# A hybrid decoder block with a planned instruction order: other durations in the planner, and late operands on TensorE

## Chip, cores and metric

One Trainium2 chip, one core. The metric is the time of one execution on the device in microseconds (us); less is better. Engines are called as the profile calls them: PE is TensorE, DVE is VectorE, ACT is ScalarE, POOL is GpSimd, SP is SyncE (it only issues DMAs here).

## What is computed

One layer over 1024 tokens of width 1024, in float32, cut to its steps:

```python
xn = rms_norm(x, norm1_g)
q, k, v, p_rw = split(xn @ w_in)                # one input projection, 3328 columns
attn = dilated_attention(q, k, v, ...)          # 8 heads of 64: three dilations, softmax merged
attn = rms_norm(attn, attn_out_g)
rwkv = rwkv7_time_mix(p_rw, ...)                # 8 heads of 64: a state of 64x64 per head, by token
x = x + concatenate([attn, rwkv]) @ w_out
xn2 = rms_norm(x, norm2_g)
return x + (silu(xn2 @ w_gate) * (xn2 @ w_up)) @ w_down     # hidden width 2816
```

## The kernel before

Matmuls with large operands are made from three products of halves: each operand is split into a high part and the rest (ACT writes `inhi`, `oph`, `woh`, ..., DVE or POOL `inlo`, `opl`, `wol`), and PE sums high x high, high x low, low x high.

The work has four stages that overlap. (1) x is loaded, normed and transposed (`xn0h`, `xn0l`, ...). (2) The input projection, `inproj`, goes through 26 column blocks for two halves of the tokens; `feed` takes each result out of PSUM. For q and k it squares (`sqf`) and scales (`qs`) with ACT, transposes the squares on PE to sum them, spreads the factors back (`exf`) and stores to DRAM (`qh_d`, `kh_d`, ...); v goes by `vf`. Beside it runs the RWKV part for eight units n (a pair of heads, half of the tokens), as streams: `decays`, `keys`, `scoring`, `sides`, `turn`, `invert`, `merge`, `chain` and `post`. `chain` is serial: for each of 8 chunks of 64 tokens in each unit (64 steps in all) PE multiplies by the state (S,ra), DVE copies the result to `Rb` (two copies), PE multiplies (Rb,M), DVE copies to `VS` and ACT to `Ub` (two copies), PE multiplies (VS,kbT and Ub,M), DVE makes the new state S (two operations), ACT reads Y out. `post` norms a unit's Y and stores it to `mix_d`; for the last unit it does so in two halves and mostly on DVE. (3) Attention: `attn_load` fetches `qv`, `kk` and `bias` for one of 16 visits to a head (two buffers), workers `attend` make scores (kk,qv), softmax (`sb`), transposes (cs,sb) and values (pt,vv). The output projection has two rounds: the first takes the RWKV results (`mixr` from `mix_d`, four of the eight row blocks of w_out, loaded by `fetch_wo` as `woraw`), the second the attention results. (4) The feed-forward part: gate and up projections and a down projection, 2928 matmuls.

No engine's order is written by hand. Each stream is a generator that yields its operations with a rank; `Flow` is a list scheduler that runs while the program is built and keeps a clock per engine (`self.clk`), and for each tile buffer when each engine will have written or read it. `ready` says when a stream's next operation could start: the engine's clock, or the end of the operations that it depends on plus a lag for the engine that they ran on (`LAG`; 60 ns more if it is to run on PE). `run` takes the operation that is ready first; among those ready by now, the one of lowest rank. `scan` estimates an operation's duration (`op.cost`) from its engine and size. `chain` has rank 3, the other RWKV streams 3.1 to 3.6, `inproj` 9: input projection matmuls are what PE does when nothing else is ready. What is planned is recorded at once in each engine's program, and on the chip each engine takes its own in that order, waiting for its operands.

What the planner may choose from also depends on where the program stands. The streams of `attn_load` are there from the start, but `fetch_wo`, `mix_load`, `mix_T` and `outproj` are added after `flow.run(rwkv)`, when every RWKV stream including `post` has been planned to its end, and the attention workers after `flow.run(dense)`, when the input projection has too:

```python
flow.run(rwkv)
...
ph3 = [flow.add(3.8, fetch_wo()), flow.add(7.4, load_wo()), flow.add(7.5, mix_load()), ...]
flow.run(dense)
...
attn += [flow.add(8.2 + 0.01 * w, attend(w)) for w in range(NW)]
```

All instructions are issued through `emit`, so every row of the profile shows that one line, and the tiles tell them apart.

Of the kernel before, what the change touches and what calls it, by code (L numbers as in the profile page):

```python
# [44 lines left out]
NFIX = C_MASK  # L45


LAG = {"PE": 200, "ACT": 145, "DVE": 140, "POOL": 65, "SP": 900}

OWN = {"PE": 0, "ACT": 100, "DVE": 130, "POOL": 95, "SP": 900}  # L50


# [4 lines left out]
class Op:  # L57


    def __init__(self, eng, name, fn, a, k):  # L60
        self.eng, self.name, self.fn, self.a, self.k = eng, name, fn, a, k
# [40 lines left out]
class Flow:  # L102
# [4 lines left out]
    def __init__(self):  # L107
        self.now, self.clk, self.marks, self.streams = 0.0, {}, {}, []
        self.slots, self.keys, self.count, self.shared = {}, {}, {}, set()
        self.free, self.weights = {}, 0.0  # L110

    def tile(self, pool, shape, dtype, name, tag=None, bufs=1):
        tag = tag or name
# [13 lines left out]
    def scan(self, op):  # L127

        def size(ap):
            n = 1  # L130
            for d in ap.shape[1:]:
                n *= d
            return n

        args = [("out" if i == 0 else "in", v) for i, v in enumerate(op.a)] + list(op.k.items())
        aps = [(k, v) for k, v in args if hasattr(v, "tensor")]
        op.wr = [self.keys[v.tensor.name] for k, v in aps if k in ("out", "accum_out") and v.tensor.name in self.keys]
        op.rd = [self.keys[v.tensor.name] for k, v in aps if k not in ("out", "accum_out") and v.tensor.name in self.keys]
        op.wr += [k for k in op.rd if k[0] in self.shared]
        n = max(size(v) for k, v in aps)  # L140
        ptr = sum(hasattr(op.k.get(k), "tensor") for k in ("scale", "bias", "scalar", "scalar1"))
        if op.eng == "PE":
            if op.name == "transpose":
                op.cost, op.m = 110, 128
            else:
                n, m, k = size(op.k["out"]), size(op.k["lhsT"]), op.k["lhsT"].shape[0]
                passes = 1 if op.k["lhsT"].dtype != F32 else PASSES if max(m, k) <= 64 else 4
                op.cost, op.m = 0.4167 * n * passes + 3, m
        elif op.eng == "SP":
            op.cost = 0  # L150
            op.bytes = 4 * max(size(v) * v.shape[0] for k, v in aps)
        elif op.eng == "POOL":
            op.cost = (280 if op.k.get("op") == ALU.pow else 100) + 93 * ptr + n * (168 if op.k.get("op") == ALU.pow else
                                            {"tensor_tensor": 2.15, "tensor_copy": 3.4}.get(op.name, 1.1))
        elif op.eng == "ACT":
            op.cost = 95 + 0.83 * n + 93 * ptr + 91 * ("accum_out" in op.k)
        else:
            op.cost = 65 + 1.04 * n + 64 * ptr

    def advance(self, s):  # L160
        while s.head is None and not s.done:
# [14 lines left out]
    def ready(self, s):  # L176
        op = s.head
        if isinstance(op, Wait):
            if any(m not in self.marks for m in op.marks):
                return None  # L180
            return max((self.marks[m] for m in op.marks), default=0.0)
        if isinstance(op, Get):
            t, n = sorted(self.free[op.kind].values()), op.n or 1
            return t[n - 1] if len(t) >= n else None
        r = self.clk.get(op.eng, 0.0)
        if op.eng == "SP":
            r = max(r, self.clk.get("queues", 0.0) - 3000)
        for keys, which in ((op.rd, 0), (op.wr, 0), (op.wr, 1)):
            for k in keys:
                if k in self.slots:  # L190
                    for e, t in self.slots[k][which].items():
                        if e != op.eng or (e == "SP" and (keys is op.rd or which)):
                            r = max(r, t + LAG[e] + (60 if op.eng == "PE" else 0))
                        elif keys is op.rd and which == 0:
                            r = max(r, t + OWN[e])
        return r

    def issue(self, s, r):
        op = s.head
        s.head = None  # L200
        if isinstance(op, Wait):
            return
        if isinstance(op, Get):
            free = self.free[op.kind]
            s.gift = sorted(free, key=free.get)[:op.n or 1]
            for tag in s.gift:
                del free[tag]
            if op.n is None:
                s.gift = s.gift[0]
            return  # L210
        start = max(r, self.now)
        if op.eng == "SP":
            self.clk["SP"] = start + 475
            end = max(start + 1125, self.clk.get("queues", 0.0)) + op.bytes / 360
            self.clk["queues"] = end
        else:
            if op.eng == "PE":

                start = max(start, self.weights + 0.833 * op.m)
                self.weights = start  # L220
            self.clk[op.eng] = end = start + op.cost
        for keys, which in ((op.rd, 1), (op.wr, 0)):
            for k in keys:
                self.slots.setdefault(k, ({}, {}))[which][op.eng] = end
        s.t = end + (LAG["SP"] if op.eng == "SP" else 0)
        self.emit(op)
# [1611 lines left out]
```

## Time and profile before

| | |
|---|---|
| median of 3 runs | 1495.26 us (1494.31 to 1502.86) |
| the profiled execution, own time | 1502.63 us |
| its span, first to last instruction | 1500.8 us |
| PE busy | 1420.0 us (95%) |
| DVE, ACT, POOL busy | 803.8, 712.8, 541.8 us |
| DMA queue q1 | 172.26 MB, 38.7% of 16 engines |
| granted PE clock, mean | 0.986 |

Busy time is summed by engine; a matmul's record overlaps the next one's, so a row's mean duration is longer than the step from one matmul to the next. A wait is idle time of an engine before an instruction, put down to what came last.

### The profile page before, as it was taken

What the parts mean: (1) busy time and instruction counts of PE and PEld (TensorE: products, weight loads), DVE (VectorE), ACT (ScalarE), POOL (GpSimd) and SP (SyncE); (2) the same over time, 40 slices, a digit from 0 to 9 for tenths busy, and PEclk for the clock granted to TensorE, in tenths of its full rate; (3) what the DMA queues carried; (4) which work ended last, traced back from release to release, by engine and by line L of the source; (5) the groups of instructions that cost most, each with busy time, mean ns of one, the idle gap of its engine ahead of it and who ended that gap; (6) DMA issues with size and microseconds to landing.
All of it is one profiled execution on the core that took longest, in us unless ns stands there. A gap on an engine that the chain in (4) does not pass through costs nothing.

```text
span 1500.8 us, 24737 instructions
## 1 busy us (share of the span) xinstructions
PE 1420.0 (95%) x8710; PEld 1142.2 (76%) x8710; DVE 803.8 (54%) x1795; ACT 712.8 (47%) x1764; POOL 541.8 (36%) x564
## 2 busy tenths in 40 slices
PE   8899999999898998899899799999999999999999
PEld 6666766677676776788777688888888888888887
DVE  4456577765655345667687744344443444334334
ACT  6434646556667766557666533333333333333332
POOL 5432344345454455133436734444444440000000
PEclk9899999999999999999999899999999999999999
DMA  6242232331422338996813222222222223445443
GB/s 201 85 128 65 67 82 78 79 96 54 126 82 89 104 116 255 249 243 159 197 37 106 73 90 83 79 78 79 79 82 85 78 85 134 147 146 198 148 147 127
DMA packets 199789, 173.83 MB, mean 116 GB/s; under 512 B 39025, under 2 KB 150897, under 8 KB 199666
## 3 DMA queue, kind: packets, MB, share of 16 engines
q1 hardware_dynamic: 199666, 172.26, 38.7%
q8 instruction: 69, 1.13, 0.3%
q14 instruction: 54, 0.44, 0.1%
HBM read 130.26 MB, written 37.75 MB: 112 GB/s over the span
## 4 chain that ended last, share of the span: by engine, by line
PE 54%; DMA 4%; DVE 3%; SPq 1%; ACT 1%; issue 1%; POOL 0%; ACTq 0%; POOLq 0%; DVEq 0%
PE bank L229 26%; PE mm L229 15%; PE chain L229 13%; DMA kk<-kl_d 2%; SPq L229 1%; DMA bias<-in_tab_dram 1%; DMA qv<-qh_d 1%; DVE acc L229 1%; DMA acc<-in_x_dram 0%; DMA mixr<-mix_d 0%; DVE tt L229 0%; DVE ml L229 0%; DVE T1l L229 0%; DVE nxn L229 0%; POOL ro L229 0%
## 5 line engine op out<-in xcount | busy, mean ns | idle before, releaser
L229 ACT ACTIVATE oph<-fraw 128x512 fp32r<-128x512 f32 x208 | 126.6, 628 | 223.4 <-PE bank L229 117.6
L229 POOL TENSOR_TENSOR opl<-fraw,oph 128x512 fp32r<-128x512 f32 x76 | 101.4, 1336 | 210.6 <-PE bank L229 110.2
L229 DVE TENSOR_TENSOR opl<-fraw,oph 128x512 fp32r<-128x512 f32 x132 | 87.7, 689 | 143.3 <-ACT oph L229 143.3
L229 ACT ACTIVATE oph<-sw 128x512 fp32r<-128x512 f32 x80 | 50.6, 632 | 178.0 <-DVE sw L229 71.9
L229 POOL TENSOR_TENSOR inlo<-inraw,inhi 128x512 fp32r<-128x512 f32 x62 | 82.1, 1325 | 110.6 <-ACT inhi L229 101.0
L229 PE MATMUL bank<-oph 128*128 128x512 f32 x176 | 68.5, 389 | 0.0
L229 PE MATMUL bank<-opl,oph 128*128 128x512 f32 x176 | 68.5, 389 | 0.0
L229 PE MATMUL bank<-oph,opl 128*128 128x512 f32 x176 | 68.5, 389 | 0.0
L229 DVE TENSOR_TENSOR opl<-sw,oph 128x512 fp32r<-128x512 f32 x80 | 56.0, 701 | 18.7 <-ACT oph L229 18.7
L229 DVE SCALAR_TENSOR_TENSOR S<-chain,ec,Sp 64x64 f32<-64x64 f32 x112 | 31.6, 282 | 51.0 <-PE chain L229 40.9
L229 DVE TENSOR_TENSOR uu<-mm,uu 128x512 f32<-128x512 f32 x20 | 13.8, 692 | 81.4 <-PE mm L229 81.4
L229 ACT ACTIVATE Ub<-chain 64x64 f32<-64x64 f32 x128 | 28.2, 220 | 56.7 <-DVE VS L229 54.9
L229 POOL TENSOR_TENSOR sw<-fraw 128x512 f32<-128x512 f32 x40 | 51.9, 1298 | 0.0
L229 ACT ACTIVATE Y<-chain 64x64 f32<-64x64 f32 x128 | 27.2, 214 | 49.2 <-DVE S L229 36.2
L229 ACT ACTIVATE inhi<-inraw 128x512 fp32r<-128x512 f32 x62 | 38.7, 624 | 14.9 <-PE mm L229 7.0
L229 DVE COPY Rb<-chain 64x64 f32<-64x64 f32 x128 | 28.9, 226 | 27.9 <-PE chain L229 25.6
L229 POOL TENSOR_TENSOR up<-up,sg 128x512 f32<-128x512 f32 x20 | 32.5, 1627 | 30.0 <-POOL sw L229 16.0
L229 ACT ACTIVATE sb<-sb,mx 128x256 f32<-128x256 f32 (+3 forms) x64 | 36.3, 569 | 7.9 <-DVE mx L229 7.5
L229 POOL TENSOR_TENSOR rsf<-smf,nhalf 128x8 f32<-128x8 f32 x16 | 27.3, 1708 | 32.3 <-DVE smf L229 26.2
L229 PE MATMUL chain<-Rb,M 128*128 128x128 f32 x128 | 27.8, 299 | 11.7 <-DVE Rb L229 11.5
L229 PE MATMUL bank<-ra,kb 64*64 64x128 f32 x512 | 38.7, 277 | 0.0
L229 PEld LDWEIGHTS chain<-Rb,M 128*128 128x128 f32 x128 | 21.0, 188 | 23.2 <-DVE Rb L229 18.9
(485 smaller groups left out, 4219.4 us busy)
## 6 DMA issues: line engine op xcount, KB each, us to landing
fraw<-in_w_down_dram SPq DMA_DIRECT2D x88, 256.0 KB, 2.8
inraw<-in_w_in_dram SPq DMA_DIRECT2D x62, 256.0 KB, 3.0
fraw<-in_w_gate_dram SPq DMA_DIRECT2D x48, 256.0 KB, 3.7
fraw<-in_w_up_dram SPq DMA_DIRECT2D x48, 256.0 KB, 3.0
fraw<-h_d SPq DMA_DIRECT2D x44, 256.0 KB, 2.9
h_d<-up SPq DMA_DIRECT2D x42, 256.0 KB, 2.1
rkv_d<-stage SPq DMA_DIRECT2D x24, 256.0 KB, 2.3
xt<-in_x_dram SPq DMA_DIRECT2D x8, 512.0 KB, 7.2
```

The source lines that it names most:

```text
L229: op.fn(*op.a, **op.k)
```

## The change

The constants and estimates of the planner. Nothing else differs; the work is the same. The lag of a DMA goes from 900 to 1500 ns. An operation on PE that depends on another engine is taken to be ready 300 ns later (LATE). Going from a matmul on the whole array to one with at most 64 rows or columns, or back, costs 100 ns in the plan (SWITCH). Single-pass matmuls are a little longer. ACT operations whose output has four dimensions (a reordering of tokens) cost 1.9 in place of 0.83 ns per element. What the code's last branch covers, DVE, starts at 80 in place of 65 ns and has other rates for scans and for four dimensions.

```diff
-LAG = {"PE": 200, "ACT": 145, "DVE": 140, "POOL": 65, "SP": 900}
+LAG = {"PE": 200, "ACT": 145, "DVE": 140, "POOL": 65, "SP": 1500}
+LATE, SWITCH = 300, 100
...
-                op.cost, op.m = 110, 128
+                op.cost, op.m, op.whole = 110, 128, True
...
-                op.cost, op.m = 0.4167 * n * passes + 3, m
+                op.cost, op.m, op.whole = (0.4375 if passes == 1 else 0.4167) * n * passes + 3, m, min(m, k) > 64
...
-            op.cost = 95 + 0.83 * n + 93 * ptr + 91 * ("accum_out" in op.k)
+            rate = 1.9 if len(op.a[0].shape) == 4 else 0.83
+            op.cost = 95 + rate * n + 93 * ptr + 91 * ("accum_out" in op.k)
         else:
-            op.cost = 65 + 1.04 * n + 64 * ptr
+            rate = {"tensor_tensor_scan": 2.2}.get(op.name, 2.0 if len(aps[0][1].shape) == 4 else 1.08)
+            op.cost = 80 + rate * n + 64 * ptr
...
-                            r = max(r, t + LAG[e] + (60 if op.eng == "PE" else 0))
+                            r = max(r, t + LAG[e] + (60 + LATE if op.eng == "PE" else 0))
...
                 start = max(start, self.weights + 0.833 * op.m)
-                self.weights = start
+                if op.whole != self.whole:
+                    start += SWITCH
+                self.weights, self.whole = start, op.whole
```

What it does to the order is shown at three places. The first is PE in the second step of the chain, from the Ub matmul to the next Rb matmul. Rows with `inhi` or `inlo` are input projection, rows with `chain` the chain step. Before:

```order
L229 MATMUL chain_1330<-Ub_117,M 128x128
L229 MATMUL mm_1415<-xn10h,inhi 128x512 x2
L229 MATMUL mm_1415<-xn10l,inhi 128x512 x4
L229 MATMUL chain_1405<-S_108,ra 128x128
L229 MATMUL mm_1415<-xn10h,inlo 128x512 x4
L229 MATMUL chain_1405<-Rb_114,M 128x128
```

And now, on PE in the same step:

```order
L235 MATMUL chain_1397<-Ub_117,M 128x128
L235 MATMUL mm_1378<-xn11l,inhi 128x512
L235 MATMUL mm_1378<-xn11h,inlo 128x512 x4
L235 MATMUL mm_1478<-xn0h,inhi 128x512 x4
L235 MATMUL mm_1478<-xn0l,inhi 128x512
L235 MATMUL chain_1451<-S_108,ra 128x128
L235 MATMUL mm_1478<-xn0l,inhi 128x512 x3
L235 MATMUL mm_1478<-xn0h,inlo 128x512 x4
L235 MATMUL chain_1451<-Rb_114,M 128x128
```

Six input projection matmuls became ten before S, and four became seven before Rb.

The second place is PE at the end of the input projection (the last row with `inlo`). `exf` and `vf` belong to q, k and v, `mixr` and `woh` to the output projection, `kk,qv` to attention scores. Before:

```order
L229 MATMUL mm_6525<-xn11h,inhi 128x512 x4
L229 MATMUL mm_6525<-xn11l,inhi 128x512
L229 MATMUL bank_6571<-cs,exf_6551 128x128 x4
L229 MATMUL mm_6525<-xn11l,inhi 128x512 x3
L229 MATMUL mm_6525<-xn11h,inlo 128x512 x4
L229 MATMUL bank_6618<-cs,mixr 128x128 x4
L229 MATMUL chain_6620<-cs,vf_6615 128x128 x4
L229 MATMUL chain_6636<-cs,mixr 128x128 x4
L229 MATMUL bank_6646<-woh_6511,mh 128x512
```

Now, on PE at that end (the chain is in its last unit, step 57 and those after it):

```order
L235 MATMUL mm_6291<-xn11h,inlo 128x512 x2
L235 MATMUL chain_6327<-VS,kbT 128x128
L235 MATMUL chain_6327<-Ub_116,M 128x128
L235 MATMUL mm_6291<-xn11h,inlo 128x512 x2
L235 MATMUL chain_6348<-S_111,ra 128x128
L235 MATMUL chain_6348<-Rb_115,M 128x128
L235 MATMUL chain_6403<-Vb_113,M 128x128
L235 MATMUL bank_6399<-cs,vf_6397 128x128 x4
L235 MATMUL chain_6348<-VS,kbT 128x128
L235 MATMUL chain_6348<-Ub_117,M 128x128
L235 MATMUL chain_6403<-S_110,ra 128x128
L235 MATMUL chain_6403<-Rb_114,M 128x128
```

The chain's last seven steps moved behind the input projection; before, all 64 stood ahead of its end.

The third place is SP's queue where the loads of w_out begin (`woraw`). `mix_d<-Y` is the store of `post`, `v_d`, `kh_d` and `kl_d` are stores of `feed`. Before:

```order
L229 DMA kh_d<-qh_6453 128x512
L229 DMA mix_d<-Y 128x2x128
L229 DMA kl_d<-qs_6359 128x512
L229 DMA kk<-kl_d 64x512 x2
L229 DMA bias<-in_tab_dram 128x512
L229 DMA woraw<-in_w_out_dram 128x512 x5
L229 DMA v_d<-v_6532 128x2x256
L229 DMA v_d<-v_6533 128x2x256
L229 DMA mixr<-mix_d 128x512 x2
```

And now, in SP's queue:

```order
L235 DMA kh_d<-qh_6372 128x512
L235 DMA kl_d<-qs_6298 128x512
L235 DMA v_d<-v_6413 128x2x256
L235 DMA v_d<-v_6414 128x2x256
L235 DMA mix_d<-Y 128x4x128
L235 DMA lgb<-in_lnx_g_dram 128x128
L235 DMA lgb<-in_lnx_b_dram 128x128
L235 DMA mix_d<-Y 128x2x128 x2
L235 DMA woraw<-in_w_out_dram 128x512 x5
L235 DMA mixr<-mix_d 128x512 x2
L235 DMA vv<-v_d 128x4x128 x3
```

The stores of k and v moved ahead of the last stores of Y, and the loads for heads (`kk`, `bias`) that stood just before the first `woraw` are further ahead; the last two `mix_d` stores now stand directly before the loads of w_out.

## Rows read from the trace of the kernel before

**Rows 1.** Stages: stretch, length, busy PE PEld DVE ACT POOL, clock, DMA, GB/s

```profile
60.00:584.00 524.00, 487.95 (x4243) 374.17 (x4241) 315.61 (x786) 305.85 (x904) 231.73 (x236) 1.00 0.33 94
584.00:671.00 87.00, 73.44 (x451) 63.47 (x452) 57.13 (x193) 50.58 (x144) 26.33 (x27) 0.96 0.94 261
671.00:850.00 179.00, 158.90 (x958) 134.04 (x958) 138.38 (x367) 117.37 (x320) 89.23 (x128) 0.97 0.47 120
850.00:1501.00 651.00, 647.10 (x2828) 532.56 (x2828) 264.59 (x399) 205.52 (x338) 167.39 (x125) 1.00 0.34 108
```

**Rows 2.** Waits of PE from 60 to 584 us: total, times, longest

```profile
PE chain L229 <- DVE Rb L229: 11.5, 15, 1.6
PE chain L229 <- ACT Ub L229: 4.0, 9, 0.8
PE bank L229 <- ACT sqf L229: 3.8, 6, 1.1
PE bank L229 <- ACT vf L229: 2.4, 5, 0.8
...
PE bank L229 <- ACT ex L229: 1.9, 3, 0.9
PE chain L229 <- DVE S L229: 1.8, 3, 0.9
```

**Rows 3.** Groups of ACT instructions, 60 to 584 us: busy, mean ns, idle before

```profile
L229 ACT ACTIVATE sqf<-mm 128x512 f32<-128x512 f32 x16 | 17.2, 1078 | 5.0 <-PE mm L229 4.5 <-issue 0.3
```

**Rows 4.** Timeline of one chain step: start, duration, instruction, idle before

```profile
139.58 0.38 PE L229 MATMUL chain<-S,ra 128*128 128x128 f32 x2
...
140.00 0.47 DVE L229 COPY Rb<-chain 64x64 f32<-64x64 f32 x2 [0.93 <-PE chain L229]
...
140.73 0.38 PE L229 MATMUL chain<-Rb,M 128*128 128x128 f32 x2
...
140.95 0.39 PE L229 MATMUL chain<-Vb,M 128*128 128x128 f32 x2
...
141.15 0.30 DVE L229 COPY VS<-chain 64x128 f32<-64x128 f32 x1 [0.69 <-PE chain L229]
141.48 0.46 ACT L229 ACTIVATE Ub<-chain 64x64 f32<-64x64 f32 x2 [0.75 <-DVE VS L229]
...
142.56 0.39 PE L229 MATMUL chain<-Ub,M 128*128 128x128 f32 x2
...
143.06 0.58 DVE L229 SCALAR_TENSOR_TENSOR S<-chain,ec,Sp 64x64 f32<-64x64 f32 x2 [1.61 <-PE chain L229]
```

**Rows 5.** Timeline of DVE, 565 to 577 us: the last post-processing

```profile
568.35 0.42 DVE L229 TENSOR_TENSOR Y<-Y,s 128x256 f32<-128x256 f32 x1
...
575.66 0.43 DVE L229 TENSOR_TENSOR Y<-Y,gt 128x256 f32<-128x256 f32 x1
```

**Rows 6.** Timeline of POOL there

```profile
571.12 1.02 POOL L229 TENSOR_TENSOR rs<-s,nhalf 128x4 f32<-128x4 f32 x1
```

**Rows 7.** Timeline of PE at the end of the input projection

```profile
582.90 1.08 PE L229 MATMUL mm<-xn11h,inlo 128*128 128x512 f32 x4
589.44 1.09 PE L229 MATMUL bank<-cs,mixr 128*128 128x128 f32 x4 [5.46 <-DMA mixr<-mix_d]
```

**Rows 8.** Stretches after idle time of PE, columns as in rows 1

```profile
588.00:592.00 4.00, 2.56 (x13) 2.59 (x13) 1.98 (x3) 2.17 (x5) 2.36 (x2) 0.61 1.05 406
704.00:720.00 16.00, 10.56 (x75) 8.32 (x73) 11.50 (x33) 14.96 (x43) 13.39 (x14) 1.00 0.50 135
720.00:724.00 4.00, 2.16 (x12) 2.13 (x12) 0.26 (x3) 0.00 (x0) 1.77 (x6) 0.75 1.07 260
```

**Rows 9.** Timeline of SP's queue at the first loads of w_out

```profile
579.35 2.33 SPq L229 DMA_DIRECT2D woraw<-in_w_out_dram  x5
...
582.96 1.33 SPq L229 DMA_DIRECT2D mixr<-mix_d  x2
```

**Rows 10.** Timeline of PE, one wait for keys of a head

```profile
617.49 0.42 PE L229 MATMUL mm<-kk,qv 128*128 128x384 f32 x1 [1.83 <-DMA kk<-kl_d]
```

More of the change, by code (lines that the diff above doesn't have):

```diff
@@ L109, in __init__ @@
         self.slots, self.keys, self.count, self.shared = {}, {}, {}, set()
-        self.free, self.weights = {}, 0.0
+        self.free, self.weights, self.whole = {}, 0.0, True
     def tile(self, pool, shape, dtype, name, tag=None, bufs=1):
```

## Prediction

> **What bounds the kernel now.** I read the stage table first, then TensorE's (PE's) list of waits, then single stretches of the timeline. The stage table [rows 1] splits the span of 1500.8 us. From 850 us on, the feed-forward stage, PE is busy for 647.1 of 651 us; no order of instructions can win there. From 60 to 584 us, where the RWKV streams run between the matmuls of the input projection, PE idles 524 - 487.95 = 36 us. From 584 to 671 us it idles 13.6 us while the DMA engines are 94% busy, and from 671 to 850 us 20.1 us. So PE bounds every stage, with holes of some 70 us before the last one, and the DMA engines share the limit from 584 to 671 us.
>
> The list of waits [rows 2] tells what the 36 us are made of: PE stood before a chain matmul for 11.5 us (operand Rb from VectorE, DVE), 4.0 us (Ub from ScalarE, ACT) and 1.8 us (S from DVE), together 17.3 us in 27 waits; and before transposes of sqf, vf and ex, written by ACT, 8.1 us in 14 waits. The rest, about 10 us, is scattered.
>
> **The change, part by part.** No instruction is added or dropped; the planner's numbers move them.
>
> *The allowance of 300 ns on PE and the corrected ACT rate.* In the first piece of order, PE gets ten input-projection matmuls between Ub and S instead of six, and seven instead of four between S and Rb. An operand that came up to 0.3 us late is then covered. For the 27 chain waits that is 27 x 0.3 = 8 us. The reorderings sqf, qs and vf were planned at 95 + 0.83 x 512 = 520 ns and now at 95 + 1.9 x 512 = 1068 ns; the row says 1078 ns [rows 3]. The 14 waits behind such results were 0.58 us on average, about the old error, so I take 6.5 of their 8.1 us. Of the scattered 10 us I take 2.5. Sum: -17 us. Bounds: 0, if DVE and ACT run just as late behind their own queues, and -36, all idle time of the stage. The wait mean of 0.64 us on the chain against an allowance of 0.3 us is why I stand near the middle. The 100 ns for a switch between small and whole matmuls and the DVE and POOL rates only shift the plan; I put them at 0 (plus or minus 2 us).
>
> *The price: the chain falls behind the input projection.* More filler per chain step uses up the filler sooner. Before, the last Rb matmul stands 66 input-projection matmuls ahead of their end. Now the input projection ends after step 57 of 64, as the second piece of order shows, and steps 58 to 64 follow each other with only eight transposes and matmuls of other streams among them. What they lack is cover; no other stream may fill it, since attention, the output projection and their loads are only added when the RWKV streams have been planned to the end.
>
> First, the last filler comes earlier. It began at 582.90 us and ended at 584.0 [rows 7]. 33 chain matmuls and 4 of gate g2 now stand behind it, at 0.22 us each (from one chain matmul's start to the next, 140.73 to 140.95 in [rows 4]), which is 8 us. With the 17 us saved it ends at 584 - 17 - 8 = 559 us.
>
> Second, a bare chain step, read off one step at 139.58 us [rows 4]: S matmul to Rb copy 0.42 us, the two copies 0.47, hop 0.05, Rb matmul to VS copy 0.42, VS copy until Ub 0.33, the two Ub copies 0.46, hop 0.05, Ub matmul until S 0.50, S 0.58, hop 0.05: 3.33 us. In the step as it ran, PE filled the gaps with input projection, so its latency cost nothing. Six steps are 20.0 us; the last one to its Ub matmul is 2.2 us, the first waits 0.6 us for S. DVE also works on the first half of the last post-processing between these steps, ten operations, of which I count 2 us as delay. Together 25 us.
>
> What the clock does there: after the 5.46 us wait at 584 us [rows 7] the granted clock was 0.61 from 588 to 592 us, and after a stretch with PE busy for 10.56 of 16 us it went from 1.00 to 0.75 [rows 8]. In the tail PE has five chain matmuls in 3.3 us, so I expect the 1.2 GHz level for part of it, and add 3 us (bounds 0 and 0.5 us on each of the three PE hops of a step, 10 us). The Trainium skill, "TensorE: Matmul & The Clock Gate", section on HAM oscillation, says that PE falls to half rate when pauses for operands lie between short bursts, and then begins each burst slow. That rule speaks against this change; the rows agree with it. By it alone the tail would be 28 to 35 us, without it 25 us.
>
> Third, what comes after the tail. The last readout of Y takes ACT about 1.2 us. Then DVE has nine operations of 0.42 us or less [rows 5], and POOL a power of 1.02 us between them [rows 6]: 4.6 us with hops. (In the row of 565 to 577 us this took 8.6 us, held up by other work, and beside the input projection it did not matter.) Only then does SyncE (SP) write mix_d, and behind it, in its queue, stand the first five loads of w_out and the loads of mixr. Before, they were issued at 579.35 and 582.96 us [rows 9]. Now: 559 + 25 + 3 + 1.2 + 4.6 + 0.8 = 593.6 us for the first. That is 14 us later. PE's scores of heads 0 and 1 already lie in this hole, 2 us of work, but they would have been hidden anyway.
>
> *From there to 671 us.* DMA bounds this stretch [rows 1]: 261 GB/s, and PE waits for halves of kk as at 617.49 us, 1.83 us [rows 10]. The third piece of order shows that the writes of v_d, kh_d and kl_d (six of 256 KB, 1.5 MB, 6 us at that rate) have left it; on the other hand PE now asks for the third head's kk 52 matmuls behind the first mixr transposes, where it was 102. I set this at 0, between -6 and +6.
>
> *From 671 to 850 us.* The 192 matmuls of the output projection's first round were used up, in PE's order, between the 12th and the 13th of the 16 visits to a head; now they last beyond the 16th. So they still cover the stretch in which the holes of 704 to 720 us lie: 16 - 10.56 = 5.4 us [rows 8]. I take 5 us for that and 2.5 us from the allowance on the other waits: -7.5 us, with bounds +5 and -20, all idle time there.
>
> Sum: +14 - 7.5 = **+6.5 us**. The profiled execution took 1502.63 us (1.8 us around its span), so 1509.1 us for one like it. It lies 7.4 us above the median of the runs, 1495.26 us; I take the difference as the same and predict 1502 us.
>
> **The rivals.** *The cover wins.* The 300 ns catch nearly every wait, because the waits come in trains: one late operand delays DVE and ACT for the next one too. For it: 15 waits on Rb, 9 on Ub, close to each other. Against it: the longest is 1.6 us. Price: 30 us saved in place of 17 (-13), and 16 instead of 7.5 later (-8.5): 6.5 - 21.5 = -15, 1480 us. It decides from 32 us saved in both stages together.
>
> *The DMA engines decide.* Issued 14 us later and with less PE work ahead of them, the loads of heads 2 to 9 arrive after PE is ready for each. For it: 0.94 busy, and waits on kk already. By SP's order 9.8 MB go out from the first w_out load to the end of the fifth head, 38 us at 261 GB/s. PE has until then some 7 us to mixr and 51,712 columns, 27 us at the 1.08 us of four times 512 [rows 7]: 34 us. Price: 4 us there and as much at two or three of the next heads, whose bytes stand as close: +14, 1516 us. Against it: 1.5 MB fewer in the stretch. It makes the kernel slower as soon as the stretch costs 9 us more than now.
>
> *The change does not do what it says.* The waits stay because DVE itself is late (S 0.58 us for two, planned at 0.43), so only 8 of the 17 us come: +15.5, 1511 us. For it: DVE's small operations are still planned too short. Against it: the corrected ACT rate is right to 1%.
>
> **How the numbers follow.** The forecast gets 0.5, the cover 0.17, the DMA 0.18, the change without effect 0.15. A measurement of this kernel can tell about 1% from no change, 15 us: below 1480.3 or above 1510.2 us. Of the forecast (own range 1492 to 1511), 0.47 lie within 1%, 0.01 below and 0.02 above; of the cover two thirds lie below, of the DMA rival 0.15 above, of the last one half above. So faster 0.12, same 0.63, slower 0.25. The range runs from 1482 to 1520 us.
>
> **What would show it.** Right: waits on sqf and vf nearly gone, those on Rb and Ub halved; the last inlo matmul near 559 us; then 30 us with PE mostly idle and seven Rb copies some 3.5 to 4 us apart; a granted clock well below 1 in that tail; mixr transposes about 12 us after the DVE operation that ends the last Y; feed-forward again about 650 us, with PE full. Wrong: the last filler at 570 us or later (no cover gained), or a tail whose steps take under 3 us, or a first w_out load before 585 us (the tail is not exposed), or PE full for good before 843 us (850 us now).

## The result, and the profile after

| | before | after |
|---|---|---|
| median of 19 runs each | 1497.37 us (1489.78 to 1502.86) | 1504.37 us (1500.64 to 1509.88) |
| ratio, 95% interval | 1 | 1.0055 [1.004, 1.0071] |
| the profiled execution, own time | 1502.63 us | 1507.61 us |
| its span | 1500.8 us | 1505.8 us |
| busy time of PE | 1420.0 us | 1428.0 us |

The kernel became 0.55% slower, 7 us by the medians; the forecast was +6.5 us. The profiled executions differ by 5.0 us. The one of before lies 5 us above its median and the one of after 3 us, so differences of a few microseconds between stages of the two are not sharp. How long an execution takes goes with the clock it was granted: of 23 later executions of before, those with a mean clock of 0.989 or more took 1490 to 1495 us, those with 0.985 or less 1495 to 1503 us.

The stages of after, cut where its stages end (columns as in [rows 1]: stretch, length, busy PE PEld DVE ACT POOL, clock, DMA share, GB/s):

```profile
0.00:60.00 60.00, 52.16 (x244) 37.70 (x245) 29.98 (x52) 34.22 (x62) 28.05 (x50) 0.94 0.50 164
60.00:545.60 485.60, 466.16 (x4158) 368.34 (x4156) 298.10 (x736) 291.98 (x833) 223.05 (x227) 0.99 0.34 100
545.60:589.80 44.20, 27.25 (x95) 21.07 (x94) 18.44 (x59) 16.82 (x72) 10.16 (x10) 0.58 0.11 36
589.80:671.00 81.20, 64.26 (x390) 56.46 (x390) 50.40 (x179) 46.25 (x135) 21.33 (x19) 0.86 0.98 270
671.00:850.00 179.00, 169.03 (x993) 142.40 (x993) 136.16 (x367) 115.35 (x319) 83.12 (x131) 0.95 0.44 116
850.00:1506.00 656.00, 649.16 (x2836) 532.75 (x2835) 270.04 (x407) 208.75 (x345) 172.94 (x129) 1.00 0.34 109
```

And the first stretch of before, which [rows 1] leave out:

```profile
0.00:60.00 60.00, 52.66 (x232) 37.94 (x233) 28.09 (x52) 33.53 (x61) 27.13 (x49) 0.86 0.50 161
```

Up to the end of the input projection, at 545.6 us in place of 584.0, PE idles 19.4 us after the first 60, where [rows 1] give 36. Then comes what before does not have: 44 us in which the clock is 0.58 and PE is busy for only 27 us, most of them at half speed. The last input projection matmuls before it:

```profile
544.90 0.71 PE L235 MATMUL mm<-xn11h,inlo 128*128 128x512 f32 x2
```

PE's waits of that first part, which answer to [rows 2] (total, times, longest):

```profile
PE chain L235 <- ACT Ub L235: 5.0, 8, 1.1
PE chain L235 <- DVE S L235: 4.8, 5, 2.0
...
PE chain L235 <- DVE Rb L235: 1.8, 4, 0.7
PE bank L235 <- ACT vf L235: 1.3, 2, 1.0
...
PE bank L235 <- ACT sqf L235: 0.4, 1, 0.4
```

Rb fell from 11.5 to 1.8 us, sqf from 3.8 to 0.4 and vf from 2.4 to 1.3. Ub did not fall (4.0 to 5.0) and S rose (1.8 to 4.8). The groups of ACT say that sqf itself takes as long as in [rows 3]; only its place in the order moved:

```profile
L235 ACT ACTIVATE sqf<-mm 128x512 f32<-128x512 f32 x16 | 17.4, 1090 | 4.1 <-PE mm L235 1.9 <-DMA qh_d<-qh 1.1 <-issue 0.5
```

The bare end of the chain, one step of the timeline without disturbance (start, duration, instruction, idle before and releaser), to be held against [rows 4]:

```profile
574.99 0.80 PE L235 MATMUL chain<-S,ra 128*128 128x128 f32 x2 [0.74 <-DVE S L235]
...
575.82 0.47 DVE L235 COPY Rb<-chain 64x64 f32<-64x64 f32 x2 [0.89 <-PE chain L235]
...
576.34 0.79 PE L235 MATMUL chain<-Rb,M 128*128 128x128 f32 x2 [0.56 <-DVE Rb L235]
...
577.17 0.30 DVE L235 COPY VS<-chain 64x128 f32<-64x128 f32 x1 [0.89 <-PE chain L235]
577.57 0.47 ACT L235 ACTIVATE Ub<-chain 64x64 f32<-64x64 f32 x2 [1.49 <-DVE VS L235]
578.08 0.80 PE L235 MATMUL chain<-VS,kbT 128*128 128x128 f32 x2 [0.52 <-ACT Ub L235]
...
578.67 0.63 PE L235 MATMUL chain<-Ub,M 128*128 128x128 f32 x2
579.41 0.58 DVE L235 SCALAR_TENSOR_TENSOR S<-chain,ec,Sp 64x64 f32<-64x64 f32 x2 [1.94 <-PE chain L235]
...
580.05 0.80 PE L235 MATMUL chain<-S,ra 128*128 128x128 f32 x2 [0.74 <-DVE S L235]
```

Every engine waits for the one before it. The step takes 5.06 us. From the S,ra matmul to the Rb copy it is 0.83 us, where [rows 4] have 0.42, and VS,kbT, which stands ahead of Ub,M, begins only when Ub is there. The granted clock in this stretch:

```profile
550.00:560.00 10.00, 6.59 (x26) 5.42 (x25) 4.52 (x12) 5.98 (x22) 3.74 (x4) 0.50 0.16 52
560.00:570.00 10.00, 5.60 (x20) 4.12 (x19) 5.08 (x16) 2.53 (x11) 2.29 (x2) 0.50 0.15 39
570.00:580.00 10.00, 6.41 (x20) 4.64 (x20) 3.36 (x12) 2.67 (x14) 0.00 (x0) 0.50 0.04 13
```

It is the 1.2 GHz level throughout. The last Ub matmul and what follows it, on PE and in SP's queue, answer to [rows 9] and [rows 7]:

```profile
583.16 0.80 PE L235 MATMUL chain<-Ub,M 128*128 128x128 f32 x2 [0.94 <-ACT Ub L235]
```

```profile
589.85 2.33 SPq L235 DMA_DIRECT2D woraw<-in_w_out_dram  x5
592.23 1.10 SPq L235 DMA_DIRECT2D mixr<-mix_d  x2
```

```profile
598.08 1.09 PE L235 MATMUL bank<-cs,mixr 128*128 128x128 f32 x4 [10.29 <-DMA mixr<-mix_d]
```

The first load of w_out is issued 10.5 us later than before (579.35), and PE waits 10.29 us for mixr instead of 5.46.

### The profile page after: what moved, and what is told of

It reads as the page before. It is cut to its first block, busy times and chain, and to the rows that moved or that the text cites. A ratio compares the mean times of both kernels' runs of the same rounds, so it can differ in the third digit from the quotient of the medians.

```text
span 1505.8 us, 24744 instructions
## 1 busy us (share of the span) xinstructions
PE 1428.0 (95%) x8710; PEld 1158.7 (77%) x8710; DVE 803.1 (53%) x1795; ACT 713.4 (47%) x1764; POOL 538.7 (36%) x564
## 5 line engine op out<-in xcount | busy, mean ns | idle before, releaser
L235 ACT ACTIVATE sb<-sb,mx 128x384 f32<-128x384 f32 (+3 forms) x64 | 36.2, 567 | 12.1 <-DVE mx L235 12.0
L235 DVE TENSOR_TENSOR up<-bank,uu 128x512 f32<-128x512 f32 x30 | 20.8, 692 | 33.9 <-PE bank L235 32.4
L235 PEld LDWEIGHTS bank<-opl,oph 128*128 128x128 f32 x176 | 33.0, 188 | 6.9
L235 PEld LDWEIGHTS bank<-oph 128*128 128x128 f32 x176 | 33.0, 188 | 6.8
L235 PEld LDWEIGHTS bank<-oph,opl 128*128 128x128 f32 x176 | 33.0, 188 | 6.8
```

What stands on the lines that cost most here:

```text
L235: op.fn(*op.a, **op.k)
```

## Experiments

Four numbers describe each run below. M is the time at which both the input projection and the chain have ended on PE (the later of the last inlo matmul's end and the last Ub matmul's end, both from the timeline of PE). The rest is the span less M. "Bare" counts the chain steps that stand behind the last input projection matmul in PE's order. The lead is the time by which the last Ub matmul ends ahead of the last inlo matmul; with a minus it ends behind it. Before has M = 582.90 + 1.08 = 584.0 and a rest of 916.8 us; after has M = 583.16 + 0.80 = 584.0 and a rest of 921.8 us. So in these two traces the gain and the price cancel at M, and the 5 us come behind it. Not all of the price is paid by M, though: from M to the first mixr transposes it is 5.5 us in before ([rows 7]) and 14.1 us in after, 8.6 us more, because the post-processing, the store and the loads that follow the chain have no cover either. From there to the feed-forward part after is 3.8 us shorter (260.5 and 256.7 us).

M and the rest are read from one traced execution of each kernel. Against the median of its session that execution lies up to 4 us lower (b_nochain) and up to 6 us higher (before, against the second session). A difference of less than 10 us between two rows of these columns therefore counts only where the ratios go the same way. The experiments ask what makes up each.

| run | estimates | allowance | bare | lead | M | rest | median us | ratio, 95% interval |
|---|---|---|---|---|---|---|---|---|
| before | old | none | 0 | 17.3 | 584.0 | 916.8 | 1497.37 | 1 |
| after | new | 300 | 7 | -38.4 | 584.0 | 921.8 | 1504.37 | 1.0055 [1.004, 1.0071] |
| late0 | new | none | 0 | 2.3 | 580.7 | 928.9 | 1507.34 | 1.008 [1.0055, 1.0105] |
| b_late300 | old | 300 | 7 | -38.5 | 587.0 | 909.3 | 1498.57 | 1.0026 [1.0006, 1.0046] |
| b_nochain | old | 300, not the chain | 0 | 5.1 | 558.2 | 906.0 | 1469.71 | 0.9821 [0.9796, 0.9847] |
| a_nochain | new | 300, not the chain | 2 | -11.2 | 578.8 | 920.4 | 1497.51 | 1.0009 [0.999, 1.0028] |
| a_warm | new | 300 | 7 | -34.4 | 580.5 | 921.5 | 1502.53 | 1.0031 [1.0005, 1.0057] |
| an_act | new, old ACT rate | 300, not the chain | 0 | 24.4 | 582.2 | 931.4 | 1511.26 | 1.0091 [1.0058, 1.0123] |
| an_dve | new, old DVE rates | 300, not the chain | 0 | 8.2 | 575.9 | 920.2 | 1499.0 | 1.0008 [0.9988, 1.0029] |
| an_sp | new, old DMA lag | 300, not the chain | 2 | -12.1 | 584.0 | 933.1 | 1521.91 | 1.0171 [1.013, 1.0213] |
| bn_pesw | old, new PE rate and switch | 300, not the chain | 0 | 53.0 | 600.0 | 908.2 | 1507.7 | 1.0079 [1.0053, 1.0106] |
| bn_rest | new, old PE rate, no switch | 300, not the chain | 10 | -53.5 | 579.6 | 931.2 | 1509.92 | 1.008 [1.0056, 1.0104] |
| bn_l150 | old | 150, not the chain | 0 | 35.7 | 580.5 | 901.2 | 1482.1 | 0.9897 [0.9864, 0.993] |
| bn_l500 | old | 500, not the chain | 0 | 11.4 | 568.5 | 901.7 | 1473.42 | 0.9838 [0.9807, 0.9869] |

Before and after were timed in a first session; the others came in three more, in the order of the table (late0 to a_nochain, a_warm to an_sp, bn_pesw to bn_l500), each with its own runs of before (medians 1496.38, 1498.79 and 1494.75 us), and each ratio is against those of its session.

### The allowance taken out, and the allowance alone

late0, the kernel after with

```diff
-LATE, SWITCH = 300, 100
+LATE, SWITCH = 0, 100
```

> After with LATE = 0, all its other estimates kept. By the order no chain step is bare (22 input projection matmuls stand behind the last Rb matmul). Theory of the bare tail: the first w_out load goes out near 580 us again (after: 589.85), PE's waits on the chain return to some 17 us between 60 us and the end of the filler, ratio to before 0.996 to 1.001. Rival, that the attention part's order and its DMAs cost the time: that part is planned with the same DMA lag and rates as in after, so the ratio stays at 1.003 to 1.006.

b_late300, the kernel before with

```diff
-                            r = max(r, t + LAG[e] + (60 if op.eng == "PE" else 0))
+                            r = max(r, t + LAG[e] + (360 if op.eng == "PE" else 0))
```

> Before with only the 300 ns allowance on PE added, DMA lag 900, old rates. By the order seven chain steps are bare, as in after. Bare tail: ratio 1.003 to 1.009, first w_out load at 588 to 595 us, granted clock about 0.5 in the tail, step near 5 us. Rival (DMA lag and attention order cost the time): 0.997 to 1.001, since the lag is the old one.

late0 gave 1.008: not faster than after (the intervals overlap), though not one chain step is bare, and outside the ranges of both readings. So the seven bare steps are not the whole of what makes after slow: the new estimates cost 0.8% without any allowance. Nor has late0 got rid of the late chain. Its last Ub matmul ends only 2.3 us ahead of the last inlo matmul, where before has 17.3 us:

```profile
578.03 0.38 PE L235 MATMUL chain<-Ub,M 128*128 128x128 f32 x2
...
580.22 0.48 PE L235 MATMUL mm<-xn11h,inlo 128*128 128x512 f32 x1
...
594.10 1.11 PE L235 MATMUL mm<-cs,mixr 128*128 128x128 f32 x4 [5.18 <-DMA mixr<-mix_d]
```

From M to the first mixr transposes PE idles 8.6 us of 13.4 in late0 and 10.3 of 14.1 in after, against 5.5 in before. A count of zero bare steps does not mean that what follows the chain is covered.

With the old estimates, the allowance alone (b_late300) brings the same seven bare steps as in after and costs 0.26%, between the ranges of its two readings. At M the bare end and the cover nearly balance with either set of estimates (b_late300 is 3.0 us later than before, after 3.3 us later than late0). In the rest the traces show the allowance gaining 7.5 us with the old estimates (916.8 to 909.3) and 7.1 us with the new ones (928.9 to 921.8). The first of these is not shown: by the two traces b_late300 would be 4.5 us faster than before, by the ratio it is 0.26% slower, since the trace of before was taken 6.3 us above the median of that session. The new estimates alone cost 12.1 us in the rest (before to late0; the ratio gives 0.8%). Of these, 7.9 us lie between M and the first mixr transposes, where the late end of the chain shows.

### The chain freed of the allowance

b_nochain, the kernel before with

```diff
-                            r = max(r, t + LAG[e] + (60 if op.eng == "PE" else 0))
+                            r = max(r, t + LAG[e] + (60 + (300 if s.rank != 3 else 0) if op.eng == "PE" else 0))
```

> Before with the 300 ns allowance for all PE operations except those of the chain stream. By the order no chain step is bare (26 input projection matmuls behind the last Rb matmul). Bare tail: the waits before transposes shrink, those on Rb, Ub and S stay near 17 us, ratio 0.993 to 0.999. Rival (the allowance does nothing for the transposes, the attention order costs): 1.000 to 1.004.

a_nochain, the kernel after with the same condition:

```diff
-                            r = max(r, t + LAG[e] + (60 + LATE if op.eng == "PE" else 0))
+                            r = max(r, t + LAG[e] + (60 + (LATE if s.rank != 3 else 0) if op.eng == "PE" else 0))
```

> After, but the chain stream is exempt from LATE. By the order two chain steps are bare in place of seven. Bare tail: five steps of 5.1 us less are bare and covered again, but the chain waits of some 10 us return; first w_out load 580 to 584 us; ratio 0.996 to 1.001. Rival (attention order and DMA lag): as after, 1.003 to 1.007.

b_nochain is 1.8% faster than before, far below the ranges of both readings, and 29 us faster than b_late300. These two differ in one condition: whether the operands of the one serial stream (rank 3) get the allowance too. Its first load of w_out, in SP's queue:

```profile
561.37 0.45 SPq L229 DMA_DIRECT2D woraw<-in_w_out_dram  x1
```

In b_late300 the first load is:

```profile
592.87 2.34 SPq L229 DMA_DIRECT2D woraw<-in_w_out_dram  x5
```

And the mixr transposes of b_nochain:

```profile
570.49 1.12 PE L229 MATMUL mm<-cs,mixr 128*128 128x128 f32 x4 [1.58 <-DMA mixr<-mix_d]
```

The stretch around M, first of b_nochain and then of b_late300, cut at the same times:

```profile
545.00:600.00 55.00, 45.96 (x260) 38.01 (x259) 33.64 (x110) 35.45 (x94) 18.26 (x16) 0.88 0.92 276
```

```profile
545.00:600.00 55.00, 30.65 (x120) 23.74 (x118) 24.18 (x84) 25.71 (x105) 11.65 (x12) 0.64 0.21 66
```

From 545 to 600 us the one has 260 matmuls at a clock of 0.88 while the DMA engines already move w_out and heads at 276 GB/s; the other has 120 at 0.64 and 66 GB/s. The first w_out load comes at 561.4 against 592.9 us, and 28.8 of these 31.5 us are in M.

Against before, M is 25.8 us earlier in b_nochain. From 60 us to M PE idles 23.9 us instead of 36.0; the waits on Rb, Ub and S are hardly less (15.6 us for 17.3). Another 11 us are PE's busy time, for as many matmuls. Some 4 us of these are the clock of the first 60 us (0.94 for 0.86, an estimate from 53 us of busy time there); what makes the others was not isolated.

With the new estimates the same condition brought only 0.5% (1.0055 to 1.0009, in the range of the bare-tail reading), and 5 us at M: two steps are still bare, and the mixr transposes still wait, as the timeline of PE in a_nochain shows (its releaser, `wol`, is what came last by the profile, not an operand of the transposes):

```profile
576.28 0.80 PE L235 MATMUL chain<-Rb,M 128*128 128x128 f32 x2 [0.58 <-DVE Rb L235]
...
593.28 1.09 PE L235 MATMUL bank<-cs,mixr 128*128 128x128 f32 x4 [10.39 <-DVE wol L235]
```

So a_nochain has to make up 20.6 us in M and 14.4 us in the rest to reach b_nochain, with nothing between the two kernels but the estimates.

### The bare end at full clock

a_warm, the kernel after with extra matmuls of the identity with itself (bf16, 128 columns) between the chain's last steps, whose result nothing uses:

```diff
+            op.cost += getattr(op, "pad", 0)
...
+    def keep():
+        yield Wait(*[("taken", len(blocks) - 1, h) for h in range(2)])
+        ps = bank("mm0")
+        w = ident.bitcast(mybir.dt.bfloat16)[:, 0:128]
+        while ("chain", 7) not in flow.marks:
+            op = PE.matmul(out=ps[:, 0:128], lhsT=w, rhs=w, start=True, stop=True)
+            op.pad = 60
+            yield op
...
+    flow.add(10, keep())
```

> The kernel after, with up to 217 extra 128x128 bf16 matmuls of the identity with itself (no result uses them) put between the chain's steps once the features are done, so that TensorE is not mostly idle in the tail; the seven bare chain steps stay. Theory T (half of the bare tail's cost is the granted clock, 0.50 of full speed in after): granted clock in the tail at least 0.85, a step of the chain 3.5 to 4.2 us against 5.06, first w_out load 6 to 11 us earlier than after's 589.85, so at 579 to 584 us, and a time of 0.994 to 0.999 of before. Rival L (the step is a chain of latencies that the clock hardly touches): step 4.7 us or more with the clock up, first w_out load within 3 us of 589.85, time 1.004 to 1.007. Rival Q (the extra matmuls stand in the way of the chain's own on TensorE): step over 5.1 us, time over 1.008.

The granted clock and one undisturbed step:

```profile
550.00:560.00 10.00, 7.48 (x85) 6.46 (x83) 4.29 (x11) 6.03 (x23) 4.18 (x5) 1.00 0.16 54
560.00:570.00 10.00, 7.17 (x83) 6.24 (x84) 6.10 (x18) 2.78 (x14) 2.42 (x2) 1.00 0.14 39
570.00:580.00 10.00, 9.28 (x110) 7.81 (x109) 3.40 (x14) 3.59 (x19) 0.00 (x0) 1.00 0.05 15
```

```profile
573.55 0.49 PE L236 MATMUL chain<-S,ra 128*128 128x128 f32 x2
...
574.08 0.47 DVE L236 COPY Rb<-chain 64x64 f32<-64x64 f32 x2 [0.58 <-PE chain L236]
...
574.60 0.49 PE L236 MATMUL chain<-Rb,M 128*128 128x128 f32 x2
...
575.13 0.29 DVE L236 COPY VS<-chain 64x128 f32<-64x128 f32 x1 [0.58 <-PE chain L236]
...
576.03 0.49 PE L236 MATMUL chain<-VS,kbT 128*128 128x128 f32 x2
576.36 0.39 PE L236 MATMUL chain<-Ub,M 128*128 128x128 f32 x2
...
576.85 0.60 DVE L236 SCALAR_TENSOR_TENSOR S<-chain,ec,Sp 64x64 f32<-64x64 f32 x2 [1.43 <-PE chain L236]
...
577.50 0.49 PE L236 MATMUL chain<-S,ra 128*128 128x128 f32 x2
```

The clock is 1.00 and the step 3.95 us against 5.06, as theory T said; but M is only 3.5 us earlier, and so is the first w_out load (586.38 against 589.85), which is neither T's 6 to 11 nor quite L's 3. The reason is in the other steps. From one S,ra matmul to the next the six steps take 6.24, 4.99, 5.58, 6.42, 3.93 and 3.95 us, 31.1 us together; in after it is 34.1 us (545.91 to 580.05). In the first four, other work, post-processing above all, stands in the queues of DVE and ACT between the chain's copies. In after, such a step on DVE and PE reads:

```profile
563.55 0.80 PE L235 MATMUL chain<-S,ra 128*128 128x128 f32 x2 [0.75 <-DVE S L235]
...
564.25 0.80 DVE L235 TENSOR_SCALAR s<-s 128x4 f32<-128x4 f32 x1 [0.75 <-ACT Y L235]
564.96 0.22 DVE L235 COPY Rb<-chain 64x64 f32<-64x64 f32 x1
565.10 0.41 DVE L235 TENSOR_TENSOR Y<-Y,s 128x256 f32<-128x256 f32 x1
565.54 0.23 DVE L235 COPY Rb<-chain 64x64 f32<-64x64 f32 x1
...
565.82 0.80 PE L235 MATMUL chain<-Rb,M 128*128 128x128 f32 x2 [1.47 <-DVE Rb L235]
```

From S,ra to Rb,M it is 2.27 us here and 1.35 us in the undisturbed step at 574.99. So of 34.1 us the clock is 3.0, the order on DVE and ACT some 7.4 (23.2 us for the first four less 4 x 3.95), and the bare latency of six steps 23.7. Most of the clock's 3.0 us lies in the last two steps, 1.1 us each; the first four took 24.0 us in after and 23.2 us here. The times of a_warm and after (1.0031 and 1.0055) have intervals that overlap; the 3.5 us are read from the traces.

### Which of the new estimates costs

Three kernels put one estimate of a_nochain back. an_act:

```diff
-            rate = 1.9 if len(op.a[0].shape) == 4 else 0.83
+            rate = 0.83
```

> As a_nochain (after with the chain freed of the allowance, 1.0009, two bare steps), with one estimate put back: ScalarE's operations on four-dimensional views cost 0.83 ns an element in the plan instead of 1.9. The order has no bare step. Theory T (what the new estimates cost is the bare end of the chain): last chain step before the last filler, first w_out load at 562 to 572 us instead of 584.70, time 0.982 to 0.992. Rival E (they cost by the order of the attention, whatever the chain does): first w_out load earlier by up to 12 us, but the stretch from it to the feed-forward part is not shorter, time 0.996 to 1.003.

an_dve:

```diff
-            rate = {"tensor_tensor_scan": 2.2}.get(op.name, 2.0 if len(aps[0][1].shape) == 4 else 1.08)
-            op.cost = 80 + rate * n + 64 * ptr
+            op.cost = 65 + 1.04 * n + 64 * ptr
```

> As a_nochain, with VectorE's old rates put back (65 + 1.04 ns an element for every operation). The order has no bare step. Theory T: as for the ScalarE rate, first w_out load at 562 to 572 us, time 0.982 to 0.992. Rival E: 0.996 to 1.003. If only one of the two (ScalarE's rate, VectorE's rates) comes out below 0.992, that estimate alone is the costly one.

an_sp:

```diff
-LAG = {"PE": 200, "ACT": 145, "DVE": 140, "POOL": 65, "SP": 1500}
+LAG = {"PE": 200, "ACT": 145, "DVE": 140, "POOL": 65, "SP": 900}
```

> As a_nochain, with the lag of a DMA put back to 900 ns. The order keeps two bare steps. Theory T (only the bare end matters): first w_out load within 3 us of 584.70, time 0.998 to 1.003. Rival S (the longer lag is what costs, by orders in which everything behind a load is put off): attention stretch 5 us or more shorter, time 0.985 to 0.996.

Theory T missed all three. an_act and an_dve have no bare step and are not faster (1.0091 and 1.0008); an_sp, which should have changed little, is the slowest of all (1.0171), with M 5.1 us later and the rest 12.7 us longer than in a_nochain. Rival E held for an_dve alone; rival S fell too. The first w_out loads came at 578.43, 578.87 and 589.83 us. No one of the three estimates is the costly one: the rest stays at 920 to 933 us whichever of them is taken back. In an_act and an_sp 6 to 7 us of it lie in the feed-forward part, where the forecast held that no order can win: from PE's last wait ahead of it to the end of the span they take 656.2 and 655.3 us against 649.4 in a_nochain, with PE busy for 652.2, 651.7 and 645.4 us on the same 2828 matmuls. Why these run slower there was not isolated.

So the two groups were tried. bn_pesw puts all three back at once; bn_rest keeps the three and puts the PE rate and the switch back:

```diff
-LATE, SWITCH = 300, 100
+LATE, SWITCH = 300, 0
...
-                op.cost, op.m, op.whole = (0.4375 if passes == 1 else 0.4167) * n * passes + 3, m, min(m, k) > 64
+                op.cost, op.m, op.whole = 0.4167 * n * passes + 3, m, min(m, k) > 64
```

> As a_nochain (1.0009), with the old estimates of DMA lag, ScalarE and VectorE put back at once: what is left of the new ones is TensorE's 0.4375 ns a column and the 100 ns for a change of tile size. It is b_nochain (0.9821) plus those two. The order has no bare chain step. Theory E (one group of estimates costs the 28 us between b_nochain and a_nochain, that of DMA, ScalarE and VectorE): 0.980 to 0.987, first w_out load at 558 to 566 us, from it to the feed-forward part 250 to 256 us. If it is the TensorE pair instead: 0.997 to 1.004. Rival O (no one estimate costs it; the greedy order falls well or badly with any shift of its numbers): in between, 0.987 to 0.997.

> As a_nochain, with TensorE's old rate and no cost for a change of tile size: it is b_nochain plus the new estimates of DMA lag, ScalarE and VectorE. The order has five bare chain steps at the end. Theory E (these three cost it): 0.998 to 1.006, first w_out load at 583 to 592 us. If the TensorE pair costs it: 0.980 to 0.988. Rival O: anything, such as five bare steps paid and the attention no longer than b_nochain's 253 us: 0.992 to 0.998.

Both come out at 1.008, against 0.9821 with neither group and 1.0009 with both, and outside every range that was named for them. For bn_rest the expectation named five bare steps; its order has ten. The columns M and rest part the two groups. bn_pesw has an M of 600.0 us and a rest of 908.2, as short as with the old estimates. Its loss is before M, and the timelines of PE and SP show where:

```profile
545.04 0.38 PE L234 MATMUL chain<-Rb,M 128*128 128x128 f32 x2
...
599.64 0.39 PE L234 MATMUL mm<-xn11h,inlo 128*128 128x512 f32 x1
```

```profile
554.79 0.98 SPq L234 DMA_DIRECT2D woraw<-in_w_out_dram  x2
```

It errs on the other side: the chain ends at 547.0 us (546.66 and 0.38 long), 53 us ahead of the input projection, which then runs until 600 us beside the first loads of w_out. bn_rest has the chain 53 us behind its last input projection matmul (526.1 to 579.6 us) and a rest of 931.2 us. In the table the rest is 920 to 933 us in every kernel with two or three of the estimates of DMA, ACT and DVE, and 901 to 917 us in every kernel without them. The split by itself proves less than it seems, since the rest also depends on how far ahead of M the loads of w_out go out: in bn_pesw 45 us and in bn_l150 24 us, so that a part of what follows is done by M. Counted from the first w_out load to the feed-forward part, these two take 303.3 and 275.5 us, as long as or longer than kernels with the three estimates (265 to 279 us). But the split holds between kernels whose first load lies at the same place. With the load 6 us behind M this stretch takes 253.3 us in b_late300, and 264.9, 265.1, 266.3, 271.9 and 273.7 us in after, a_nochain, a_warm, an_sp and bn_rest; with the load 3 us behind M it takes 252.8 us in b_nochain and 267.8 us in an_dve. And b_nochain and bn_rest differ in these three estimates alone: 906.0 and 931.2 us of rest. Without an allowance no such difference is shown: 270.6 us in before, 271.5 us in late0. So it is shown that, beside an allowance, the three together lengthen what follows M; by which order of instructions they do it was not isolated. One thing goes with it: summed over stretches of 4 us as busy time of PE times what the granted clock lacks to 1.00, PE loses some 6 to 10 us to the clock between the first w_out load and the feed-forward part in the kernels without the three estimates (bn_pesw 12), and 10 to 17 us in those with them.

### The size of the allowance

bn_l150 and bn_l500 are b_nochain with another number:

```diff
-                            r = max(r, t + LAG[e] + (60 + (300 if s.rank != 3 else 0) if op.eng == "PE" else 0))
+                            r = max(r, t + LAG[e] + (60 + (150 if s.rank != 3 else 0) if op.eng == "PE" else 0))
```

> As b_nochain (the kernel before, 300 ns of allowance on every TensorE operand except the chain's; 0.9821), with 150 ns. No bare chain step. Theory A (allowance off the chain gains through covered waits and an early end of the chain, and that varies smoothly with its size): 0.981 to 0.990. Rival O (b_nochain is a lucky order): 0.992 to 1.005, with the first w_out load after 572 us or an attention stretch of 262 us or more.

> As b_nochain, with 500 ns. No bare chain step. Theory A: 0.978 to 0.988, first w_out load at 558 to 568 us, from it to the feed-forward part 248 to 257 us. Rival O: 0.992 to 1.005.

0.9897, 0.9821 and 0.9838 for 150, 300 and 500 ns: all three faster than before, all in the time range of theory A, so b_nochain is not one lucky value of the allowance. It is still a sensitive order: bn_pesw, with another rate and a switch cost for PE and nothing else, is 38 us slower. And bn_l150 shows one sign of rival O, 275.5 us from the first w_out load to the feed-forward part, because its load goes out 24 us ahead of M. The interval of bn_l150 lies above that of b_nochain; the one of bn_l500 overlaps it. By M and rest the three are not smooth (580.5, 558.2, 568.5 and 901.2, 906.0, 901.7): with 150 ns the chain ends first, at 544.8 us, and the input projection 36 us later. b_nochain, at 1469.71 us, is the fastest kernel of this study, 1.8% ahead of before and 35 us ahead of after.

## Why the prediction was right, step by step

*The time.* Forecast +6.5 us and 1502 us; measured 1504.37 us, ratio 1.0055. It lies in the likeliest case, but that is in part luck: two terms in it were mis-sized and cancelled, and the new estimates' own effect on the order was set at nothing. Without an allowance they cost 0.8% (late0), some 11 us, more than the whole sum. With it they cost about 0.3% (1.0026 for b_late300, 1.0055 for after), so the two parts of the change do not add up.

*The cover, -17 us: right as a sum.* Idle time of PE from 60 us to the end of the input projection went from 36.0 to 19.4 us, -16.6. Its parts were not: Rb gave 9.7 us and S took back 3 and Ub 1, so the chain gave 5.7 us for the 8 forecast; sqf and vf gave 4.5 for 6.5; and the scattered waits more than 6 for 2.5.

*The last input projection matmul at 559 us: 13 us too late.* It ended at 545.6. The work moved behind it, 8 us, was about right. By the counts, 232 + 4243 matmuls had started by the old end and 244 + 4158 by the new one, 73 fewer, 66 of them of the chain; these go in pairs, 0.22 us a pair in [rows 4], and in before the matmuls that moved took 10 us from one start to the next. But PE's busy time up to that end is 22.3 us less (540.6 and 518.3 us). The other 12 us, which the forecast did not have, are matmuls that follow each other faster: the 1272 of the input projection go from 259 to 253 ns from one start to the next, idle time taken off, which is 7 us. An estimate of 4 of the 12 us is the stretch up to 60 us, with a clock of 0.94 instead of 0.86 on 52 us of busy time. That need not be the order's doing, since a_warm, whose plan is the same there, had 0.91. What made the others was not isolated.

*The tail, 28 us: 10 us too short.* From 545.6 us to the end of the last Ub matmul it is 38.4 us. The clock's 3 us were right (3.0 in six steps, 3.5 at the first w_out load). The step was wrong: 3.33 us were read off a step whose holes other matmuls filled, and 3.95 us is a bare one at full clock, since VS,kbT starts after Ub and ahead of Ub,M (0.33 us, left out of the sum) and each pair of matmuls takes 0.53 to its reader instead of 0.42. That is 3.7 us in six steps. The other work of DVE and ACT cost 7.4 us in place of 2, and the last step some 1.7 more than its 2.2. The granted clock was 0.50 from 550 to 580 us. The forecast's 28 to 35 us for the tail fell short all the same, because the clock is the smallest of the three parts of these six steps. The Trainium skill, "TensorE: Matmul & The Clock Gate", section on HAM oscillation, spoke of bursts that begin slow; the trace agrees that PE fell to half rate, but it shows no fall and rise from burst to burst: the clock stayed at 0.50.

*The first w_out load at 593.6 us: 589.85.* The early end of the filler and the longer tail cancel to 3.7 us. From the last Ub matmul to the load it was 5.9 us for 6.6.

*From there to the feed-forward part, -7.5 us: about right, but not by the gain named.* Between the first w_out load and the last wait of PE ahead of feed-forward (849.91 us before, 854.77 after) it went from 270.6 to 264.9 us, -5.6. The forecast named one gain there. With the allowance alone (b_late300) the same stretch takes 253.3 us, 17 us less than before by these traces, and the new estimates on top of it (after) take back 11.6 us; of that loss nothing was foreseen. The step that failed is "The 100 ns for a switch between small and whole matmuls and the DVE and POOL rates only shift the plan; I put them at 0 (plus or minus 2 us)", together with the DMA lag of 1500 ns, which got no term at all, and the ACT rate, which was counted as a gain only. A plan that is shifted is another order.

*The signs.* The seven last Rb copies were to come 3.5 to 4 us apart; they are 5.1 to 6.6 us apart. The mixr transposes were to come 12 us after the DVE operation that ends the last Y; it was 8.8 us. None of the signs of being wrong appeared.

*Rivals.* The DMA engines did not decide: PE's waits for kk between the first w_out load and feed-forward are 9.6 us in both traces, and feed-forward took 650.9 and 651.0 us from the last wait ahead of it. The cover did not win in this kernel. b_nochain comes out below that rival's 1480 us, but its waits on the chain stay, so it does not get there by the rival's mechanism. The change did what it said to the waits on sqf and Rb.

## What to carry to other kernels

An allowance for late operands belongs on the streams that have slack. On a serial stream it makes the planner put more filler into each step, the filler runs out before the stream does, and the end is paid in bare latency: here one condition was worth 29 us of 1500 with the old estimates and 7 us with the new ones. It is no guarantee: bn_rest spares the chain the allowance and still has ten bare steps. Before judging a planner's change by the waits that it removes, look at which of the filler and the longest chain ends last, and by how much. What follows the chain is covered only as far as the chain ends ahead of the filler; in after it takes 14 us from the last Ub matmul to the first mixr transposes, and late0, 2.3 us ahead, had no bare step and still paid. A long lead alone is no gain either: bn_pesw, 53 us ahead, is slower than before. An untested way is to let the loads of w_out and the attention into the plan before the RWKV streams have ended. And estimates that are better one by one need not make a better greedy order; they are to be measured singly and together.

## What the runs showed of the hardware

PE with five short pairs of matmuls in 5 us was granted the 1.2 GHz level for all of 30 us (0.50 in each stretch of 10 us of after), and with some 30 more small matmuls per step, in a_warm, 1.00. The lower level lengthened an undisturbed chain step from 3.95 to 5.06 us, not to twice: from a pair's start to its reader it is 0.83 instead of 0.53 us, while the copies on DVE and ACT keep their 0.47 us.
